# A conv feed-forward stage: one PSUM tile for each product accumulator, and casts, gelu and low parts issued at another distance from their users

## The chip, the cores and the metric

The kernel runs on one core of one Trainium2 chip. The metric is the time of one execution on the device in microseconds (us). Engines are named as in the profile: PE (TensorE, matmuls), PEld (its weight loads), DVE (VectorE), ACT (ScalarE), POOL (GpSimd; here it only issues transfers that add onto their target) and SP (SyncE, which issues plain transfers).

## The reference, cut to what matters

One layer of a diffusion backbone on 128 context tokens and 512 latent tokens, 640 in all, with a model width of 1024. Only the second half of the layer, the convolutional feed-forward, is touched:

```python
def _conv_ffn(h, w_up, w_dw, b_dw, w_down, latent):
    a, g = jnp.split(h @ w_up, 2, axis=-1)      # w_up (1024, 2 * 2816)
    ...                                         # conv: 3x3 depthwise on the latent grid, width 3 on the context
    conv = conv + b_dw
    return (jax.nn.gelu(conv) * g) @ w_down     # w_down (2816, 1024)

def _layer(x, cond, latent, s0_f, s0_b, alpha, p):
    ...                                         # token mixers, first norm, modulation: h2
    f = _conv_ffn(h2, p['w_up'], p['w_dw'], p['b_dw'], p['w_down'], latent)
    x = _layer_norm(alpha * x + g2 * f.astype(x.dtype), p['ln2_g'], p['ln2_b'])
```

## The kernel before

Activations lie with channels on partitions and the 640 tokens along the free axis. The 2816 channels are 22 tiles of 128, numbered j. For each j the stage needs an `a` and a `g` tile. Every operand of a product is kept as a rounded high part and a low part (what the rounding left), and a product is three matmuls (`mm3`, L277 to L279): high by high, high by low, low by high. The high part is a cast on ACT, the low part a subtraction on DVE (`low`, L195); `split` makes both, one right behind the other.

**Pairs.** Tiles 4 to 21 go through `up_pair`, which computes `a` and `g` of one j together with seven half-size products in place of eight (a Strassen-Winograd form on 512-row halves of the weights and 320-token halves of the activations). Each product is 12 matmuls of 128x320. Three accumulators take them: `xx` (products 1, 3, 5 and 7, all summed onto one another, with a copy to SBUF after each), `yy` (product 2) and `vv` (products 4 and 6). `xx` and `yy` are the two banks of one two-bank tile `pp`, `vv` is a one-bank tile. Between products the function issues the copies (ACT), the sums (DVE), a few operations of an older tile's convolution (`pump`) and one step of the weight preparation (`advance`).

**Weights.** A pair needs four quarters, named `a`, `c`, `r` and `t`, each split into a high tile `wh` and a low tile `wl`, with four buffers each. Pair j prepares the quarters of pair j + 1, one after the second, fourth, sixth and seventh product. The sums of weights that the seven products need are made by transfers: SP loads the raw tiles `ra` and `rb` of a pair (`load_pair`, called when `t` of the pair two before has been split) and a raw tile for `r`, and POOL issues transfers that add: two onto `rb`, then `ra[s] += rb[s]` when `a` has been split, from which `t` is cast. There are four such raw tiles (`sraw`), so two pairs' worth. A queue's transfers are issued in program order, and POOL's wait for the transfers before them where they read their result.

**Convolution.** `feed(j)` queues the operations of a tile's depthwise convolution: `begin` (an activation on ACT), ten taps on DVE, `close` (the gelu on ACT), then `gated` (a multiplication on DVE and a cast on ACT) and `rest` (the low part on DVE). `pump(n)` issues n of them. A pair issues 12, and a convolution has 12, so the queue keeps the length that it had.

**Down-projection.** After tiles 7, 9 and 14 a block (`down_part`) multiplies finished tiles by `w_down` and adds the result onto `x1d` in DRAM through POOL; it also prepares the next pair's quarters. Blocks for tiles 0 to 3, 4 to 7 and 8 to 13 stand between pairs; that for 14 to 21 comes last.

The order of instructions on all five engines is the order of the program text in this stage (a manual schedule), so where a line stands decides what it waits behind.

Of the kernel before, what the change touches and what calls it, by code (L numbers as in the profile page):

```python
# [18 lines left out]
P = 128  # L19
# [134 lines left out]
def layer_kernel(ctx, tc, wst, wada, par, cst, ftab, ttab, cond, x, state, sgub, wst_t, rows, bg, y, snew):  # L154
# [1386 lines left out]
    with tc.tile_pool(name="pu", bufs=1, reuse_waits="tile") as pu:  # L1541
        def onto(o, i):
            nc.gpsimd.dma_start(out=o, in_=i, accum_op=ALU.add)
# [34 lines left out]
        def next_pair():  # L1578
            if rest_pair:
                load_pair(rest_pair.pop(0))  # L1580

        def entry(key):
            kind, *a_ = key
            if kind == "a":
                ra, rb = pairs[a_[0]]
                got_w[key] = split(ra)
                onto(ra[:, s_], rb[:, s_])
            elif kind == "c":
                got_w[key] = split(pairs[a_[0]][1])
            elif kind == "t":  # L1590
                got_w[key] = split(pairs.pop(a_[0])[0][:, s_], 512)
                next_pair()
            else:
                w = got_w[key] = split(raws.pop(key))
                if kind == "d":
                    got_w[key] = halves(w)
                next_raw()

        def advance():
            if entries:  # L1600
                entry(entries.pop(0))
# [18 lines left out]
        def feed(j, at):  # L1620
# [23 lines left out]
            def close():  # L1644
                cv = hold["cv"]
                A.activation(cv, cv, AF.Gelu_apprx_tanh)  # L1646
                tail_q.extend([gated, rest])
                age[0] = 0

            def gated():  # L1650
# [15 lines left out]
        def pump(n):  # L1666
            while n and (taps_q or tail_q):
                if tail_q and (age[0] >= 2 or not taps_q):
                    tail_q.pop(0)()
                    age[0] = 0  # L1670
                else:
                    f = taps_q.pop(0)
                    f()
                    if f.__name__ in ("begin", "close"):
                        continue
                    age[0] += 1
                n -= 1

# [4 lines left out]
        def up_pair(j):  # L1683
            at = a, g = up_tiles(j)
            wa, wc, wr, wt = [(e, j) for e in "acrt"]
            pp = ppt("up")
            xx, yy, vv = pp[:, 0, 0:320], pp[:, 1, 0:320], p1t("up")[:, 0:320]

# [10 lines left out]
            V.tensor_tensor(a[:, near], a[:, near], yy, op=ALU.add)  # L1699
            pump(1)  # L1700
            product(xx, wc, 512, s2, 0)
            A.copy(g[:, near], xx)
# [3 lines left out]
            advance()  # L1706
            pump(1)
            product(xx, wr, 0, s3, 0)
            A.copy(g[:, far], xx)
# [5 lines left out]
            V.scalar_tensor_tensor(g[:, near], g[:, near], -1.0, vv, op0=ALU.mult, op1=ALU.subtract)  # L1715
            pump(1)
            product(xx, wt, 0, a22, 0)
            A.copy(a[:, far], xx)
            advance()
            pump(3)  # L1720
            feed(j, at)

        def up_one(j):
            at = up_tiles(j)
            for i in range(2):
                pp = ppt("up")
                for _ in proj_steps(pp, std[i], h2):
                    pass
                A.copy(tv(at[i]), pv(pp))
                pump(5)  # L1730
                advance()
            feed(j, at)

        def down_part(n):
# [5 lines left out]
            for nh in range(2):  # L1740
                for t in range(NT):
# [10 lines left out]
                    onto(x1d[t][:, c], ftmp)  # L1752
                    pump(rate)

        def contract(pr, ws, t, c0, cn, accum=None):
# [18 lines left out]
        with tc.manual_schedule(engines=MANUAL3 | {mybir.EngineType.Pool, mybir.EngineType.SP}):  # L1774
# [5 lines left out]
            advance()  # L1780
            advance()
            next_raw()
            for kind, n in jobs:
# [6 lines left out]
            while entries:  # L1790
                advance()
            for t in range(4):
                load_acc(t)
# [104 lines left out]
```

## Time and profile before

| | us |
|---|---|
| median of 3 runs (1368.27 to 1371.88) | 1370.25 |
| the profiled execution | 1375.1 |
| its span | 1373.3 |
| PE busy | 1225.7 |
| DVE busy | 892.0 |
| ACT busy | 512.6 |
| POOL busy | 91.9 |

The span is cut into 40 slices of 34.3 us on the page. The page's line of the granted clock gives, for each slice, the share of TensorE's full clock that it was allowed. The feed-forward's pairs run from 804 to 1304 us of the span.

### The profile page before, as it was taken

What the parts mean: (1) busy time and instruction counts of PE and PEld (TensorE: products, weight loads), DVE (VectorE), ACT (ScalarE), POOL (GpSimd) and SP (SyncE); (2) the same over time, 40 slices, a digit from 0 to 9 for tenths busy, and PEclk for the clock granted to TensorE, in tenths of its full rate; (3) what the DMA queues carried; (4) which work ended last, traced back from release to release, by engine and by line L of the source; (5) the groups of instructions that cost most, each with busy time, mean ns of one, the idle gap of its engine ahead of it and who ended that gap; (6) DMA issues with size and microseconds to landing.
All of it is one profiled execution on the core that took longest, in us unless ns stands there. A gap on an engine that the chain in (4) does not pass through costs nothing. (4 is left out here: it accounts for less than half of the span.)

```text
span 1373.3 us, 19086 instructions
## 1 busy us (share of the span) xinstructions
PE 1225.7 (89%) x7535; PEld 1151.2 (84%) x7535; DVE 892.0 (65%) x1656; ACT 512.6 (37%) x844; POOL 91.9 (7%) x111
## 2 busy tenths in 40 slices
PE   8999999999999999999999957888876897676897
PEld 7999999999999998999888856867776776675776
DVE  6697576486774858884678556675645553555586
ACT  5576363343433222322356333424233322333330
POOL 0000000000000000000000021021321022211000
PEclk9999999999999999999999968898986799676799
DMA  8412121121351525443432355575764347533242
GB/s 320 174 66 74 63 77 47 66 66 62 108 190 48 191 97 175 138 154 109 151 108 93 100 122 130 140 136 137 130 152 124 101 107 145 129 90 91 63 144 92
DMA packets 54970, 161.80 MB, mean 118 GB/s; under 512 B 6232, under 2 KB 8664, under 8 KB 54880
## 3 DMA queue, kind: packets, MB, share of 16 engines
q1 hardware_dynamic: 39472, 131.22, 28.0%
q0 software_dynamic: 15408, 29.37, 12.8%
q8 instruction: 59, 0.97, 0.3%
q14 instruction: 31, 0.25, 0.1%
HBM read 136.97 MB, written 14.16 MB: 110 GB/s over the span
## 5 line engine op out<-in xcount | busy, mean ns | idle before, releaser
L195 DVE TENSOR_TENSOR wl<-raw,wh 128x1024 fp32r<-128x1024 f32 x123 | 148.1, 1205 | 105.8 <-ACT wh L219 104.6
L277 PE MATMUL up<-go,wh 128*128 128x320 f32 (+2 forms) x384 | 138.4, 361 | 67.9 <-ACT fm L1695 60.3
L219 ACT CAST wh<-raw 128x1024 fp32r<-128x1024 f32 x119 | 122.8, 1034 | 198.3 <-PE gm L278 91.5
L277 PEld LDWEIGHTS up<-go,wh 128*128 128x128 f32 x384 | 87.2, 227 | 74.3 <-ACT fm L1695 65.1
L195 DVE TENSOR_TENSOR wl<-sraw,wh 128x1024 fp32r<-128x1024 f32 (+1 forms) x54 | 56.3, 1045 | 134.9 <-ACT wh L219 134.8
L278 PE MATMUL up<-go,wh 128*128 128x320 f32 (+2 forms) x384 | 134.3, 350 | 1.1 <-DVE go L195 1.1
L279 PE MATMUL up<-go,wl 128*128 128x320 f32 (+2 forms) x384 | 133.7, 348 | 0.5 <-DVE wl L195 0.5
L277 PE MATMUL up<-s,wh 128*128 128x320 f32 x216 | 79.9, 370 | 54.5 <-DVE fm L1699 54.5
L277 PE MATMUL gm<-h,wh 128*128 128x320 f32 x384 | 121.4, 316 | 0.0
L278 PE MATMUL gm<-h,wh 128*128 128x320 f32 x384 | 118.9, 310 | 0.0
L279 PE MATMUL gm<-h,wl 128*128 128x320 f32 x384 | 118.6, 309 | 0.0
L1641 DVE SCALAR_TENSOR_TENSOR cv<-fm,par,cv 128x441 f32<-128x441 f32 (+2 forms) x152 | 105.3, 692 | 2.3
L277 PEld LDWEIGHTS up<-s,wh 128*128 128x128 f32 x216 | 49.1, 227 | 60.8 <-DVE fm L1699 60.8
L421 DVE SCALAR_TENSOR_TENSOR adac<-rawa,csil,adac 128x512 f32<-128x512 f32 x120 | 84.8, 745 | 10.8 <-DMA rawa<-in_wada 8.8
L278 PEld LDWEIGHTS up<-go,wh 128*128 128x128 f32 x384 | 87.0, 227 | 2.4 <-DVE go L195 2.0
L279 PEld LDWEIGHTS up<-go,wl 128*128 128x128 f32 x384 | 86.0, 224 | 0.8 <-DVE wl L195 0.8
L219 ACT CAST wh<-sraw 128x1024 fp32r<-128x1024 f32 (+1 forms) x54 | 48.8, 905 | 82.6 <-DMA sraw<-sraw 30.9
L279 PE MATMUL up<-s,wl 128*128 128x320 f32 x216 | 77.1, 357 | 0.0
L278 PE MATMUL up<-s,wh 128*128 128x320 f32 x216 | 77.1, 357 | 0.0
L277 PE MATMUL dn<-wh,h 128*128 128x512 f32 (+1 forms) x188 | 72.6, 386 | 3.1 <-ACT h L1654 3.0
L279 PE MATMUL dn<-wh,h 128*128 128x512 f32 (+1 forms) x188 | 72.0, 385 | 1.9 <-DVE h L195 1.7
L277 PEld LDWEIGHTS gm<-h,wh 128*128 128x128 f32 x384 | 72.1, 188 | 1.7 <-issue 1.2
(454 smaller groups left out, 3283.6 us busy)
## 6 DMA issues: line engine op xcount, KB each, us to landing
raw<-in_wst SPq DMA_DIRECT2D x134, 512.0 KB, 3.6
sraw<-in_wst SPq DMA_DIRECT2D x36, 512.0 KB, 4.9
rawa<-in_wada SPq DMA_DIRECT2D x32, 512.0 KB, 3.5
sraw<-sraw POOLq DMA_DIRECT2D x36, 256.0 KB, 3.4
wa<-in_wada SPq DMA_DIRECT2D x16, 512.0 KB, 7.4
x1d<-ftmp POOLq DMA_DIRECT2D x30, 256.0 KB, 4.0
sraw<-in_wst POOLq DMA_DIRECT2D x18, 256.0 KB, 4.1
raw<-in_wst POOLq DMA_DIRECT2D x18, 256.0 KB, 4.4
```

The lines of the kernel that those rows point to most:

```text
L195: V.tensor_tensor(out, src, hi.bitcast(F32), op=ALU.subtract)
L219: A.copy(wh[:, 0:n], r)
L277: PE.matmul(out, lhsT=l[0], rhs=r[0], start=start, stop=False, skip_group_check=onto)
L278: PE.matmul(out, lhsT=l[0], rhs=r[1], start=False, stop=False, skip_group_check=onto)
L279: PE.matmul(out, lhsT=l[1], rhs=r[0], start=False, stop=stop, skip_group_check=onto)
L421: MAC.scalar_tensor_tensor(acc_[:, cd], r[:, i], s_, acc_[:, cd], op0=ALU.mult, op1=ALU.add)
L1641: V.scalar_tensor_tensor(cg[:, r0:r1, c0:c1], ag[:, r0 + r - 1:r1 + r - 1, c0 + c - 1:c1 + c - 1], tap(r, c), cg[:, r0:r1, c0:c1], op0=ALU ...
```

## The change

`up_pair` takes `xx` from a two-bank tile as before, but `yy` from a one-bank tile of its own, as `vv`. `split` is no longer used for the pairs' quarters: `cast` issues the cast on ACT at once and puts the low part, with the transfers that follow it, into a list; `settle` issues what is in the list. `settle` is called at the start of each `advance` and at fixed places of `up_pair`, ahead of the next product. The gelu becomes an operation of the tail queue (`curve`) that is issued when three operations have gone by since the last tap, or at once when there are no taps left; the distance of `gated` and `rest` stays two. `begin` of the next tile is issued one tap earlier where the next entry of the queue is the last.

```diff
--- before.py
+++ after.py
@@ -1579,24 +1579,40 @@
             if rest_pair:
                 load_pair(rest_pair.pop(0))
 
+        lows = []
+
+        def cast(r, n=1024):
+            wh = strm.tile([P, 1024], F32R, tag="wh", bufs=4, name=nm("wh"))
+            wl = strm.tile([P, 1024], F32R, tag="wl", bufs=4, name=nm("wl"))
+            A.copy(wh[:, 0:n], r)
+            return (wh, wl), lambda: low(wl[:, 0:n], r, wh[:, 0:n])
+
         def entry(key):
             kind, *a_ = key
             if kind == "a":
                 ra, rb = pairs[a_[0]]
-                got_w[key] = split(ra)
-                onto(ra[:, s_], rb[:, s_])
+                got_w[key], f = cast(ra)
+                after = lambda: onto(ra[:, s_], rb[:, s_])
             elif kind == "c":
-                got_w[key] = split(pairs[a_[0]][1])
+                got_w[key], f = cast(pairs[a_[0]][1])
+                after = lambda: None
             elif kind == "t":
-                got_w[key] = split(pairs.pop(a_[0])[0][:, s_], 512)
-                next_pair()
+                got_w[key], f = cast(pairs.pop(a_[0])[0][:, s_], 512)
+                after = next_pair
             else:
-                w = got_w[key] = split(raws.pop(key))
-                if kind == "d":
-                    got_w[key] = halves(w)
-                next_raw()
+                w, f = cast(raws.pop(key))
+                got_w[key] = halves(w) if kind == "d" else w
+                after = next_raw
+            lows.append((f, after))
+
+        def settle():
+            while lows:
+                f, after = lows.pop(0)
+                f()
+                after()
 
         def advance():
+            settle()
             if entries:
                 entry(entries.pop(0))
 
@@ -1642,10 +1658,11 @@
                                        tap(r, c), cg[:, r0:r1, c0:c1], op0=ALU.mult, op1=ALU.add)
 
             def close():
-                cv = hold["cv"]
-                A.activation(cv, cv, AF.Gelu_apprx_tanh)
-                tail_q.extend([gated, rest])
+                tail_q.extend([(curve, 3), (gated, 2), (rest, 2)])
                 age[0] = 0
+
+            def curve():
+                A.activation(hold["cv"], hold["cv"], AF.Gelu_apprx_tanh)
 
             def gated():
                 cv = hold["cv"]
@@ -1665,15 +1682,20 @@
 
         def pump(n):
             while n and (taps_q or tail_q):
-                if tail_q and (age[0] >= 2 or not taps_q):
-                    tail_q.pop(0)()
+                if tail_q and (age[0] >= tail_q[0][1] or not taps_q):
+                    f = tail_q.pop(0)[0]
+                    f()
                     age[0] = 0
+                    n -= f.__name__ != "curve"
+                    continue
                 else:
                     f = taps_q.pop(0)
                     f()
                     if f.__name__ in ("begin", "close"):
                         continue
                     age[0] += 1
+                    if len(taps_q) > 1 and taps_q[1].__name__ == "begin":
+                        taps_q.pop(1)()
                 n -= 1
 
         def up_tiles(j):
@@ -1683,8 +1705,8 @@
         def up_pair(j):
             at = a, g = up_tiles(j)
             wa, wc, wr, wt = [(e, j) for e in "acrt"]
-            pp = ppt("up")
-            xx, yy, vv = pp[:, 0, 0:320], pp[:, 1, 0:320], p1t("up")[:, 0:320]
+            xx = ppt("up")[:, 0, 0:320]
+            yy, vv = (p1t("up")[:, 0:320] for _ in range(2))
 
             def product(o, w, c0, acts, new):
                 w = got_w[w]
@@ -1698,6 +1720,7 @@
             advance()
             V.tensor_tensor(a[:, near], a[:, near], yy, op=ALU.add)
             pump(1)
+            settle()
             product(xx, wc, 512, s2, 0)
             A.copy(g[:, near], xx)
             pump(2)
@@ -1705,6 +1728,7 @@
             A.copy(a[:, far], vv)
             advance()
             pump(1)
+            settle()
             product(xx, wr, 0, s3, 0)
             A.copy(g[:, far], xx)
             pump(1)
@@ -1714,10 +1738,12 @@
             advance()
             V.scalar_tensor_tensor(g[:, near], g[:, near], -1.0, vv, op0=ALU.mult, op1=ALU.subtract)
             pump(1)
+            settle()
             product(xx, wt, 0, a22, 0)
             A.copy(a[:, far], xx)
             advance()
             pump(3)
+            settle()
             feed(j, at)
 
         def up_one(j):
@@ -1729,6 +1755,7 @@
                 A.copy(tv(at[i]), pv(pp))
                 pump(5)
                 advance()
+                settle()
             feed(j, at)
 
         def down_part(n):
@@ -1751,6 +1778,7 @@
                     V.scalar_tensor_tensor(ftmp, p1, 1.0 / ALPHA, g2[:, cd, c], op0=ALU.mult, op1=ALU.mult)
                     onto(x1d[t][:, c], ftmp)
                     pump(rate)
+                    settle()
 
         def contract(pr, ws, t, c0, cn, accum=None):
             cd = 0 if t == 0 else 1
@@ -1779,6 +1807,7 @@
                 feed(j, [landed.pop((j, i)) for i in range(2)])
             advance()
             advance()
+            settle()
             next_raw()
             for kind, n in jobs:
                 {"one": up_one, "pair": up_pair, "down": down_part}[kind](n)
@@ -1789,6 +1818,7 @@
                         low(lo, s1_[k], hi)
             while entries:
                 advance()
+            settle()
             for t in range(4):
                 load_acc(t)
             ln = [[mt()[:, 0:512] for _ in range(2)] for _ in range(2)]
```

Three places show how instructions move. In the names `up` is a product accumulator, `go` and `s` are activations, `wh` and `wl` the weights' parts, `cv` the convolution's tile, `fm` the `a` and `g` tiles, `raw` and `sraw` the weights' raw tiles, `ftmp` an evicted block of the down-projection; the number behind the name tells buffers apart.

PE, pair 20, at the end of its first and the start of its second product; before:

```order
L278 MATMUL up_11332<-go_7642,wh_11230 128x320
L279 MATMUL up_11332<-go_7641,wl_11231 128x320
L277 MATMUL up_11332<-go_7689,wh_11230 128x320
L278 MATMUL up_11332<-go_7690,wh_11230 128x320
L279 MATMUL up_11332<-go_7689,wl_11231 128x320
```

and now:

```order
L278 MATMUL up_11348<-go_7642,wh_11246 128x320
L279 MATMUL up_11348<-go_7641,wl_11247 128x320
L277 MATMUL up_11349<-go_7689,wh_11246 128x320
L278 MATMUL up_11349<-go_7690,wh_11246 128x320
L279 MATMUL up_11349<-go_7689,wl_11247 128x320
```

The order is the same; the second product writes a tile of its own.

DVE, the end of pair 19 and the start of pair 20, from the low part of `r` on (L195 with `raw`); before:

```order
L195 TENSOR_TENSOR wl_11299<-raw_11022,wh_11298 128x1024
L1715 SCALAR_TENSOR_TENSOR fm_11198<-fm_11198,up_11200 128x320
L1641 SCALAR_TENSOR_TENSOR cv_11214<-fm_11057,par,cv_11214 128x448
L195 TENSOR_TENSOR wl_11320<-sraw_11044,wh_11319 128x512
L1641 SCALAR_TENSOR_TENSOR cv_11214<-fm_11057,par,cv_11214 128x7x63
L1652 TENSOR_TENSOR cv_11214<-cv_11214,fm_11058 128x640
L195 TENSOR_TENSOR h_11327<-cv_11214,h_11326 128x640
L1633 SCALAR_TENSOR_TENSOR cv_11347<-fm_11197,par,cv_11347 128x127 x2
L195 TENSOR_TENSOR wl_11364<-sraw_11184,wh_11363 128x1024
L1699 TENSOR_TENSOR fm_11330<-fm_11330,up_11332 128x320
```

and now (the gate is L1669, the first taps L1649, the add of `yy` L1721):

```order
L195 TENSOR_TENSOR wl_11315<-raw_11038,wh_11314 128x1024
L1657 SCALAR_TENSOR_TENSOR cv_11230<-fm_11071,par,cv_11230 128x7x63
L1669 TENSOR_TENSOR cv_11230<-cv_11230,fm_11072 128x640
L195 TENSOR_TENSOR h_11342<-cv_11230,h_11341 128x640
L195 TENSOR_TENSOR wl_11336<-sraw_11065,wh_11335 128x512
L1649 SCALAR_TENSOR_TENSOR cv_11364<-fm_11212,par,cv_11364 128x127 x2
L1721 TENSOR_TENSOR fm_11346<-fm_11346,up_11349 128x320
L1657 SCALAR_TENSOR_TENSOR cv_11364<-fm_11212,par,cv_11364 128x7x63
L195 TENSOR_TENSOR wl_11381<-sraw_11206,wh_11380 128x1024
```

The low part of `t` (L195 with `sraw`, 128x512) stood ahead of the last tap, the gate and the low part of `h`, and stands behind them; the low part of the next `a` (the last `wl` row) stood ahead of the add of `yy` and stands behind it and a tap. ACT's order at this place is the same as before: copy of product 7, cast of `t`, gelu, cast of `h`, copy of the next product 1.

POOL, the end of the third down-projection block and the start of pair 15; before:

```order
L1543 DMA raw_10633<-in_wst 128x512
L1543 DMA sraw_10647<-in_wst 128x512
L1543 DMA sraw_10647<-sraw_10647 128x512
L1543 DMA x1d_7123<-ftmp_10652 128x512
L1543 DMA sraw_10226<-sraw_10227 128x512
```

and now:

```order
L1543 DMA raw_10650<-in_wst 128x512
L1543 DMA x1d_7123<-ftmp_10656 128x512
L1543 DMA sraw_10661<-in_wst 128x512
L1543 DMA sraw_10661<-sraw_10661 128x512
L1543 DMA sraw_10243<-sraw_10244 128x512
```

The block's last output accumulate (`x1d` from `ftmp`) stood between the two accumulates onto `rb` and `ra[s] += rb[s]`, and now stands ahead of all three.

## Rows read from the trace of the kernel before

**Rows 1.** The page's granted clock of TensorE, 40 slices, tenths.

```profile
PEclk9999999999999999999999968898986799676799
```

**Rows 2.** Waits of PE, 804 to 1306 us: waiter, releaser: total us, times, longest.

```profile
PE up L277 <- ACT fm L1695: 60.3, 18, 8.7
PE up L277 <- DVE fm L1699: 54.5, 18, 4.5
```

**Rows 3.** Windows between casts of t: length, busy time by engine, PEclk, DMA share, GB/s.

```profile
803.94:865.56 61.62, 46.60 (x244) 45.15 (x245) 36.19 (x56) 24.91 (x40) 9.60 (x11) 0.77 0.49 117
1010.37:1027.44 17.07, 13.43 (x79) 13.17 (x80) 9.58 (x14) 6.52 (x10) 3.53 (x4) 0.90 0.64 146
1168.71:1186.76 18.05, 14.53 (x76) 14.13 (x77) 9.13 (x14) 6.41 (x10) 3.10 (x4) 0.78 0.53 116
1027.44:1073.67 46.23, 32.90 (x167) 31.57 (x166) 25.28 (x39) 15.76 (x24) 6.11 (x7) 0.74 0.43 108
1186.76:1257.92 71.16, 51.18 (x254) 49.18 (x253) 38.58 (x58) 23.62 (x37) 10.49 (x12) 0.71 0.46 111
916.42:939.05 22.63, 16.97 (x84) 16.33 (x84) 15.49 (x23) 7.70 (x13) 4.36 (x5) 0.77 0.62 136
991.00:1010.37 19.37, 15.54 (x84) 14.88 (x84) 7.30 (x10) 5.68 (x10) 4.39 (x5) 0.82 0.75 166
1143.11:1168.71 25.60, 15.86 (x96) 15.07 (x94) 9.03 (x11) 5.80 (x10) 5.64 (x7) 0.89 0.68 151
865.56:885.73 20.17, 15.15 (x83) 14.61 (x82) 12.36 (x20) 7.54 (x13) 1.73 (x2) 0.83 0.54 154
939.05:957.34 18.29, 13.78 (x73) 13.51 (x74) 10.76 (x17) 7.28 (x11) 1.73 (x2) 0.81 0.58 168
1073.67:1097.17 23.50, 16.83 (x83) 16.16 (x82) 12.54 (x20) 7.56 (x13) 1.73 (x2) 0.71 0.45 133
1257.92:1303.79 45.87, 32.55 (x167) 31.21 (x166) 25.42 (x39) 15.44 (x25) 0.86 (x1) 0.74 0.17 52
```

**Rows 4.** Timeline, end of pair 18, ACT, DVE and PE: start, duration, line, idle before.

```profile
1234.12 0.62 ACT L219 CAST wh<-sraw 128x512 fp32r<-128x512 f32 x1
...
1236.92 0.74 ACT L1646 ACTIVATE cv<-cv 128x640 f32<-128x640 f32 x1 [2.18 <-DVE cv L1641]
...
1237.69 0.83 DVE L1652 TENSOR_TENSOR cv<-cv,fm 128x640 f32<-128x640 f32 x1 [0.80 <-ACT cv L1646]
...
1238.55 0.72 ACT L1654 CAST h<-cv 128x640 fp32r<-128x640 f32 x1 [0.89 <-DVE cv L1652]
...
1239.18 0.42 ACT L1695 COPY fm<-up 128x320 f32<-128x320 f32 x1
...
1239.31 0.83 DVE L195 TENSOR_TENSOR h<-cv,h 128x640 fp32r<-128x640 f32 x1 [0.79 <-ACT h L1654]
...
1239.65 0.64 PE L277 MATMUL up<-go,wh 128*128 128x320 f32 x1 [4.14 <-ACT fm L1695]
```

**Rows 5.** Windows: one product after a gap, and two products late in a pair.

```profile
1239.65:1243.15 3.50, 3.50 (x12) 3.17 (x12) 1.18 (x3) 0.93 (x2) 0.94 (x2) 0.50 0.73 178
1254.08:1257.60 3.52, 3.52 (x26) 3.52 (x25) 3.48 (x6) 1.48 (x2) 0.00 (x0) 1.00 0.00 0
```

**Rows 6.** Timeline, pairs 10 and 11, SP, POOL and ACT.

```profile
1011.74 0.33 SPq L1560 DMA_DIRECT2D sraw<-in_wst  x1
...
1017.54 0.87 POOL L1543 DMA_DIRECT2D sraw<-in_wst  x1 [3.55 <-DVE cv L1641]
1022.54 1.79 POOL L1543 DMA_DIRECT2D sraw<-sraw  x2 [4.13 <-DMA sraw<-in_wst]
...
1027.44 0.62 ACT L219 CAST wh<-sraw 128x512 fp32r<-128x512 f32 x1 [0.34 <-DMA sraw<-sraw]
```

**Rows 7.** Transfers, 804 to 1306 us: issues, KB each, median us to landing.

```profile
raw<-in_wst SPq DMA_DIRECT2D x34, 512.0 KB, 3.6
sraw<-sraw POOLq DMA_DIRECT2D x33, 256.0 KB, 3.4
```

## The prediction

> **What bounds the kernel now.** I read the slices of the page first [rows 1]: TensorE is granted its full clock for 23 of 40 slices and then, from about 790 us on, between 0.6 and 0.9 of it. That second part is the feed-forward stage, and there TensorE waits in every one of its 18 pair steps at the same two places [rows 2]: before the second product of a pair for ACT's copy at L1695 (60.3 us in all) and before the third product for DVE's add at L1699 (54.5 us). Both waits come from one tile: `xx` and `yy` lie in the two halves of `pp`, so a write to one half waits for a read of the other.
>
> I then cut the stage at the casts of the quarter `t`, the last of the four weight quarters that a pair prepares for the next (S(j) is the cast for pair j). These marks are used below because a loop runs from one to the next. [rows 3] gives the 18 steps: 389.6 us together, 21.6 us a pair. One product is 12 matmuls, 1.76 us at 2.4 GHz and 3.50 us at 1.2 GHz [rows 5], so seven full-speed products are 12.3 us, and 9.3 us a pair are waiting or slow clock. The row of the two products after 1254.08 has the clock at 1.00, the row right after a 4.14 us gap has 0.50.
>
> The late pairs show why the copy comes so late [rows 4]: ACT casts `t` at 1234.12, then the gelu waits for the last convolution tap on DVE, the gate on DVE waits for the gelu, the cast of `h` on ACT waits for the gate, and only then, at 1239.18, ACT gets to the copy. TensorE resumes at 1239.65.
>
> **The change, part by part.** *Tiles.* `yy` gets its own one-bank tile. Product 2 no longer waits for the copy, and product 3 no longer for the add; it still waits for the copy, since it accumulates onto `xx`, but product 2 now lies between. Work removed or added: none (the counts on TensorE, ACT, POOL and SP are unchanged, and DVE's seven extra listed rows are taps no longer listed together). The second one-bank tile per pair takes one of four rotating buffers; its former holders were evicted a pair or some blocks earlier, so I price it at nothing; if the cover failed, the price would be one wait for DVE, at most the 54.5 us / 18 = 3.0 us a pair of [rows 2].
>
> *Casts and low parts.* Each low part now stands a tap later on DVE, after the add instead of ahead of it. The four prepared quarters are used a whole pair later, so TensorE does not see it. It does matter for transfers: in the late pairs the order rows show `t`'s low part behind the gate and the low part of `h`. The load of the second raw tile `rb` of pair j+2 overwrites what this low part reads, so it starts later.
>
> *Gelu.* In the late pairs ACT's order at the pair's end is unchanged: the queue of taps is empty by then, so `curve` is issued at once, without its three operations of distance. The chain of [rows 4] stays, though it now delays product 3, not product 2.
>
> So something else has to bound a pair, and I see three candidates. TensorE: 12.3 us. DVE: 38.58 us busy in three pairs, 12.9 a pair [rows 3], plus the gaps that its own order keeps, 0.80 for the gelu and 0.79 for the cast of `h` [rows 4] and about 0.3 for the next opening activation: 14.8 us. And a loop through the transfers: the cast of `t` needs `ra[s] += rb[s]`; POOL issues that only after both accumulates onto the `rb` of the pair after; these need that `rb` loaded; the load needs the previous `t`'s low part. Where the kernel before runs into this loop it can be read off [rows 6]: cast 1010.37, load of `rb` issued 1011.74, first accumulate 1017.54, second 1022.54, the third behind it at 1022.54 + 0.90, and the next cast starts on its landing at 1027.44. That is 17.07 us: 1.37 + 5.80 + 5.00 + 0.90 + 4.00. The other late steps, 22.5 to 23.9 us, hide it.
>
> With the new order of DVE, the first term grows. From the cast of `t`: 0.65 to the gelu, 0.77 to the gate (1236.92 to 1237.69), 0.86 to the cast of `h`, 0.76 to its low part, 0.75 until `t`'s low part starts and 0.68 that it takes: 4.5 us. The second term shrinks, because the loads ahead of `rb` are done by then: a load by itself lands after 3.6 us (median of the 512 KB raw loads, [rows 7]). Sum 4.5 + 3.65 + 5.00 + 0.90 + 4.00 = 18.05 us. With the load still at 5.80 it is 20.2; with the last landing at its median of 3.4 [rows 7] it is 17.4. I take 18.05, as the load then is nearest to one by itself. TensorE fits in: product 3 starts about 4.2 us after the cast, and products 3 to 7 take 3.50 + 2.9 + 3 x 1.76 = 11.7 us if the gap slows the first two, together 15.9.
>
> By the Trainium skill (DMA: Bandwidth & Descriptors, section on the anatomy of one DMA) a transfer costs about 2.0 us plus its bytes at 436 GB/s: 3.2 us for 512 KB and 2.6 us for 256 KB. By that estimate the loop would be 4.5 + 3.2 + 2.6 + 0.9 + 2.6 = 13.8 us and would bind nothing, which is the first rival below; the rows have 4.0 and 5.0 us for these 256 KB accumulates, and the measurement decides.
>
> The steps of [rows 3], before and after:
> - Five steps in which the loop and the late chain act together (1027.44 to 1073.67 and 1186.76 to 1257.92): 117.4 us, then 5 x 18.05 = 90.3. Gain 27.1.
> - Five steps with no gelu between cast and low part (three in 803.94 to 865.56, 1010.37 to 1027.44, 1168.71 to 1186.76): 96.7 us, then the loop as it was, 5 x 17.0. Gain 11.7.
> - Three steps from a down-projection block: 67.6 us. The last output accumulate now stands ahead of the weights' accumulates on POOL, not between them (order rows), which takes one transfer out of the loop; but `t`'s low part stands behind that block's eviction and, at pairs 8 and 10, two taps. Bounds: nothing, and 3 x 18 = 54, a gain of 13.6. I take 3, near the low end, because the two shifts oppose each other.
> - Five steps outside the loop, since no `t` behind them waits for a pair's load (865.56 to 885.73, 939.05 to 957.34, 1073.67 to 1097.17, and two in 1257.92 to 1303.79): 107.8 us. The first two keep no gelu in front of the copy: cast 0.62, opening activation 0.92, copy 0.42, 0.5 to restart, then five products, 8.8 us fast and 12.3 with two of them slow: 11.3 to 14.8, taken as 13 each. The other three take DVE's 14.8. Sum 70.4, gain 37.4.
>
> Total gain 79.2 us. The profiled execution took 1375.1 us for a span of 1373.3, 4.85 above the runs' median of 1370.25; the same distance below 1375.1 - 79.2 = 1295.9 gives **1291 us**. Down-projection blocks, the part before 804 us and the tail are taken as unchanged, since none of the two waits lies there and no product is added or moved.
>
> **The rivals.** *The transfers are quicker and the loop binds nothing.* Then DVE's 14.8 us bounds the first kind too (74 us), about 14 the second (70), the third gains its 13.6: 43.4 + 26.7 + 13.6 + 37.4 = 121.1, time 1249. For it: the loop's figures come from a stretch with DMA busy at 0.64, the late pairs have 0.43 to 0.46 [rows 3]. Against it: quicker pairs raise that share.
>
> *The loop gets longer*, because loads and accumulates crowd together: 20.2 us in the first kind, nothing gained in the second and third: 16.4 + 37.4 = 53.8, time 1317. For it: the 5.80 us in [rows 6].
>
> *TensorE stays at 1.2 GHz.* The only long gap per pair would now lie before product 3; if the clock fell there and did not come back within the pair, seven products would take 24.5 us and a pair some 25.5: 18 x 25.5 - 389.6 = 69 us slower, about 1440. It decides from 21.6 us a pair on. Against it: before the change two gaps a pair still leave 0.71 to 0.74 in these steps [rows 3], and the clock is back at 1.00 by the sixth product [rows 5].
>
> *The change does nothing*: product 3 waits for the same copy and takes over the whole wait. For it: the chain of [rows 4] is not shortened. Against it: product 2 now runs inside that wait, and the add's wait has no successor.
>
> **How the numbers follow.** My forecast 0.55 (1275 to 1308 for itself), quick transfers 0.25, long loop 0.13, no effect 0.03, slow clock 0.04. The range of 1250 to 1318 reaches to the first rival's time and to the long loop's; what it leaves out is half of the quick case and the last two. A measurement of this kernel tells about 0.3% from no change: faster 0.93, same 0.03, slower 0.04.
>
> **What would show it.** Right: no TensorE wait between a pair's first and second product; one wait per pair, before the third, for ACT's copy, of 2 to 3 us in the late pairs; ACT's cast of `t` waiting for `ra[s] += rb[s]` in most steps; casts of `t` 17 to 19 us apart; the load of `rb` issued some 4.5 us after the cast. Wrong: casts of `t` that wait for TensorE or DVE alone (the loop does not bind), steps of 20 us or more, a granted clock below 0.7 in the late steps, or down-projection blocks that change by more than 2 us.

## The result and the profile after

The changed kernel takes 1299.35 us (median of 4 runs, 1294.89 to 1306.42) against 1371.07 us for the kernel before (4 runs): a ratio of 0.948, 95% interval 0.9424 to 0.9536. Five more runs in another session gave 1306.41 us and 0.9502 (0.948 to 0.9524). The forecast was 1291 us with a range of 1250 to 1318. The profiled execution of the changed kernel took 1306.42 us (span 1304.6), 68.7 less than that of before; all sums below are made against this one.

The page's granted clock, and the waits of PE and ACT (waiter, line, releaser: total us, times, longest us), which answer to [rows 1, 2]:

```profile
PEclk9999999999999999999999997799898889888989
```

```profile
PE up L277 <- ACT fm L1717: 88.8, 17, 10.8
...
ACT wh L1587 <- DMA sraw<-sraw: 101.5, 15, 12.8
```

Two kinds of wait of 18 each have become one: nothing waits between a pair's first and second product, nothing waits for the add, and the third product waits for the copy of the first (L1717). That wait is longer than either was. The row of ACT says why: ACT's casts wait 101.5 us for landings of `sraw<-sraw`, and the copy stands on ACT behind the cast of `t`.

The twelve windows of [rows 3], between the same casts, in the same order:

```profile
799.80:856.47 56.67, 43.04 (x252) 42.38 (x252) 39.78 (x61) 23.32 (x39) 9.57 (x11) 0.83 0.56 132
994.37:1014.41 20.04, 14.62 (x84) 14.36 (x84) 11.12 (x17) 6.40 (x11) 3.52 (x4) 0.84 0.56 129
1130.10:1147.28 17.18, 14.98 (x84) 14.72 (x84) 11.12 (x17) 6.41 (x10) 2.63 (x3) 0.82 0.63 148
1014.41:1052.28 37.87, 27.93 (x168) 27.40 (x168) 25.09 (x38) 15.52 (x25) 5.23 (x6) 0.86 0.54 130
1147.28:1206.68 59.40, 42.27 (x249) 41.74 (x250) 37.78 (x57) 23.30 (x36) 10.46 (x12) 0.83 0.56 127
903.23:924.24 21.01, 14.12 (x84) 13.86 (x84) 15.45 (x23) 7.05 (x13) 3.48 (x4) 0.85 0.64 155
971.06:994.37 23.31, 12.74 (x86) 12.32 (x84) 7.30 (x9) 5.58 (x10) 5.39 (x7) 0.90 0.75 163
1109.57:1130.10 20.53, 15.80 (x108) 15.53 (x106) 7.28 (x9) 5.79 (x9) 5.24 (x6) 0.99 0.82 183
856.47:867.38 10.91, 9.23 (x62) 9.10 (x62) 9.40 (x15) 7.14 (x11) 0.87 (x1) 1.00 0.75 216
924.24:937.55 13.31, 11.70 (x61) 11.69 (x62) 9.33 (x16) 7.24 (x11) 1.73 (x2) 0.72 0.62 170
1052.28:1067.24 14.96, 11.71 (x61) 11.71 (x62) 10.88 (x18) 7.33 (x11) 1.73 (x2) 0.70 0.53 157
1206.68:1233.24 26.56, 22.34 (x150) 21.80 (x149) 22.66 (x36) 15.12 (x23) 0.85 (x1) 1.00 0.26 75
...
sum 321.75, PE 240.48 PEld 236.61 DVE 207.20 ACT 130.22 POOL 50.68; mean PE 20.04 PEld 19.72 DVE 17.27 ACT 10.85 POOL 4.22
```

The 18 steps take 321.75 us, 67.8 less than before, and that is nearly all of the 68.7. The remaining 0.9 is a balance: up to the first cast 4.1 less, the three down-projection blocks between pairs 1.4 more (111.69 against 110.29; the first grew by 5.2, the third shrank by 3.6), the tail 1.9 more.

Two turns of the loop on ACT, SP, POOL, DVE and PE, which answer to [rows 4, 6]: from the cast of `t` for pair 5 to that for pair 6, and from that for pair 17 to that for pair 18 and the third product behind it:

```profile
819.26 0.62 ACT L1587 CAST wh<-sraw 128x512 fp32r<-128x512 f32 x1 [6.10 <-DMA sraw<-sraw]
...
820.63 0.33 SPq L1560 DMA_DIRECT2D sraw<-in_wst  x1
...
828.91 0.87 POOL L1543 DMA_DIRECT2D sraw<-in_wst  x1 [8.07 <-DMA sraw<-in_wst]
833.33 1.75 POOL L1543 DMA_DIRECT2D sraw<-sraw  x2 [3.54 <-DMA sraw<-in_wst]
...
840.35 0.62 ACT L1587 CAST wh<-sraw 128x512 fp32r<-128x512 f32 x1 [7.61 <-DMA sraw<-sraw]
...
1147.28 0.62 ACT L1587 CAST wh<-sraw 128x512 fp32r<-128x512 f32 x1 [4.26 <-DMA sraw<-sraw]
...
1151.69 0.33 SPq L1560 DMA_DIRECT2D sraw<-in_wst  x1
1162.12 0.33 SPq L1569 DMA_DIRECT2D raw<-in_wst  x1
...
1156.78 0.87 POOL L1543 DMA_DIRECT2D sraw<-in_wst  x1 [6.79 <-DVE cv L1657]
1161.11 1.76 POOL L1543 DMA_DIRECT2D sraw<-sraw  x2 [3.46 <-DMA sraw<-in_wst]
1167.17 0.86 POOL L1543 DMA_DIRECT2D raw<-in_wst  x1 [4.30 <-DMA raw<-in_wst]
...
1167.88 0.62 ACT L1587 CAST wh<-sraw 128x512 fp32r<-128x512 f32 x1 [6.48 <-DMA sraw<-sraw]
...
1169.17 0.82 DVE L1669 TENSOR_TENSOR cv<-cv,fm 128x640 f32<-128x640 f32 x1 [6.48 <-ACT cv L1665]
...
1170.66 0.42 ACT L1717 COPY fm<-up 128x320 f32<-128x320 f32 x1
...
1171.13 0.63 PE L277 MATMUL up<-s,wh 128*128 128x320 f32 x1 [6.68 <-ACT fm L1717]
```

The second turn, read as the prediction read it: 4.41 from the cast to the load of `rb`, 5.09 to the first accumulate, 4.33 to the second, 0.88 to the third (the second of the `x2` row, taken at half of it), and 5.89 until the cast starts on its landing: 20.60 us. The row of the first accumulate names DVE as its releaser; by the trace the load of `rb` lands at 1156.20, which is when POOL's wait ends, and the row starts 0.58 us later. The load of `r` (L1569) is issued 0.13 us after the third accumulate and moves beside it. ACT, DVE and PE all stand still until the landing. The first turn, with the low part of `t` early, has 1.37, 8.28, 4.42, 0.88 and 6.14 us, together 21.09. Transfers from 800 to 1236 us (issues, KB each, median us to landing) against the second of [rows 7]; the accumulates have gone from 3.4 to 4.4:

```profile
sraw<-sraw POOLq DMA_DIRECT2D x33, 256.0 KB, 4.4
```

### The profile page after: what moved, and what is told of

It reads as the page before. It is cut to its first block, busy times and chain, and to the rows that moved or that the text cites. A ratio compares the mean times of both kernels' runs of the same rounds, so it can differ in the third digit from the quotient of the medians.

```text
span 1304.6 us, 19072 instructions
## 1 busy us (share of the span) xinstructions
PE 1184.2 (91%) x7535; PEld 1116.2 (86%) x7535; DVE 887.8 (68%) x1656; ACT 509.9 (39%) x844; POOL 91.7 (7%) x111
## 5 line engine op out<-in xcount | busy, mean ns | idle before, releaser
L195 DVE TENSOR_TENSOR wl<-raw,wh 128x1024 fp32r<-128x1024 f32 x123 | 148.0, 1204 | 84.9 <-ACT wh L219 75.9
L277 PE MATMUL up<-s,wh 128*128 128x320 f32 x216 | 76.8, 356 | 88.8 <-ACT fm L1717 88.8
L219 ACT CAST wh<-raw 128x1024 fp32r<-128x1024 f32 x83 | 85.0, 1027 | 168.3 <-PE gm L278 91.6
L277 PE MATMUL up<-go,wh 128*128 128x320 f32 (+2 forms) x384 | 124.2, 323 | 7.3 <-ACT fm L1755 6.3
L278 PE MATMUL up<-go,wh 128*128 128x320 f32 (+2 forms) x384 | 123.1, 321 | 1.0 <-DVE go L195 1.0
L279 PE MATMUL up<-go,wl 128*128 128x320 f32 (+2 forms) x384 | 122.3, 318 | 0.4 <-DVE s11hv L307 0.4
L195 DVE TENSOR_TENSOR wl<-sraw,wh 128x1024 fp32r<-128x1024 f32 (+1 forms) x54 | 56.3, 1043 | 73.5 <-ACT wh L1587 73.1
L1587 ACT CAST wh<-sraw 128x1024 fp32r<-128x1024 f32 (+1 forms) x54 | 48.7, 903 | 127.4 <-DMA sraw<-sraw 101.5
L277 PEld LDWEIGHTS up<-go,wh 128*128 128x128 f32 x384 | 76.8, 200 | 8.8 <-ACT fm L1755 6.6
L278 PEld LDWEIGHTS up<-go,wh 128*128 128x128 f32 x384 | 76.2, 199 | 2.4 <-DVE go L195 2.0
L279 PEld LDWEIGHTS up<-go,wl 128*128 128x128 f32 x384 | 75.8, 197 | 0.8 <-DVE s11hv L307 0.8
L278 PE MATMUL up<-s,wh 128*128 128x320 f32 x216 | 74.2, 343 | 0.0
L279 PE MATMUL up<-s,wl 128*128 128x320 f32 x216 | 73.9, 342 | 0.0
L277 PEld LDWEIGHTS gm<-h,wh 128*128 128x128 f32 x384 | 72.1, 188 | 1.7 <-issue 1.2
```

The costliest lines, as they stand in the source:

```text
L195: V.tensor_tensor(out, src, hi.bitcast(F32), op=ALU.subtract)
L219: A.copy(wh[:, 0:n], r)
L277: PE.matmul(out, lhsT=l[0], rhs=r[0], start=start, stop=False, skip_group_check=onto)
L278: PE.matmul(out, lhsT=l[0], rhs=r[1], start=False, stop=False, skip_group_check=onto)
L279: PE.matmul(out, lhsT=l[1], rhs=r[0], start=False, stop=stop, skip_group_check=onto)
L1587: A.copy(wh[:, 0:n], r)
```

## The experiments

My theory: the changed kernel's steps are set by the transfer loop, and TensorE's remaining wait is only where this shows. Rivals: the tiles or the order alone set what is gained, or the landings are slow wherever they stand. Ratios are to the kernel before in the same session.

**The two halves of the change, each alone.** The edit of the first run, in the kernel before:

```diff
-            pp = ppt("up")
-            xx, yy, vv = pp[:, 0, 0:320], pp[:, 1, 0:320], p1t("up")[:, 0:320]
+            xx = ppt("up")[:, 0, 0:320]
+            yy, vv = (p1t("up")[:, 0:320] for _ in range(2))
```

> The kernel before with only the three product accumulators of a pair in tiles of their own; casts, gelu and low parts stay in the old order. Theory: the late steps of the changed kernel are set by the transfer loop (cast of t, low part of t, load of the right half, three accumulating transfers, landing), and in the old order the low part of t stands right behind its cast, 0.6 + 0.7 us instead of 4.4 us, so a late step is 20.8 - 3.1 = 17.7 us unless the old order's waits between ScalarE and VectorE hold it: 1265 to 1290 us, below the changed kernel. Rival, the order carries part of the gain: without it the waits of VectorE for casts and gelu keep the add and the evictions late, and the steps stay over 19 us in every pair: 1305 to 1340 us.

Measured: 1310.54 us, ratio 0.9566 (0.9542 to 0.9591).

The second run takes the same lines back out of the changed kernel.

> The changed kernel with the first two products of a pair back in the two halves of one tile; the new order of casts, gelu and low parts stays. Theory: the second and the third product wait again for the copy and the add, TensorE keeps falling to half clock, and the gain is lost: 1345 to 1375 us. Rival, the order by itself brings the copy and the add so much earlier that the shared tile costs little: 1300 to 1330 us.

Measured: 1312.28 us, ratio 0.9582 (0.9552 to 0.9612). Both times lie in the rivals' ranges: each half alone gives some 60 us, and both together, by the ratios, only 0.6 to 1.0% more. The first rival's mechanism did not show: with the tiles alone the steps do not stay over 19 us everywhere. Three late ones, from the cast for pair 17 to that for pair 20, take 51.01 us, where the changed kernel has 59.40 in the windows above:

```profile
1157.69:1208.70 51.01, 40.65 (x236) 40.12 (x237) 37.73 (x56) 23.60 (x36) 10.49 (x12) 0.83 0.63 145
```

Waits in the tiles-only kernel and then in the order-only kernel:

```profile
ACT wh L219 <- DMA sraw<-sraw: 72.1, 12, 12.7
...
PE up L277 <- ACT fm L1695: 67.9, 14, 10.6
```

```profile
ACT wh L1587 <- DMA sraw<-sraw: 45.2, 12, 12.0
...
PE up L277 <- DVE fm L1721: 11.7, 18, 1.2
```

In both, ACT's casts wait for landings (45.2 and 72.1 us; before it was 30.9). In the second the tile is still shared, yet the wait for the add has fallen from the 54.5 of [rows 2] to 11.7.

**Which part of the order.** In the order-only kernel, gelu and opening activation go back to their old places; only the low parts stay later:

```diff
-                tail_q.extend([(curve, 3), (gated, 2), (rest, 2)])
+                cv = hold["cv"]
+                A.activation(cv, cv, AF.Gelu_apprx_tanh)
+                tail_q.extend([gated, rest])
...
-                    if len(taps_q) > 1 and taps_q[1].__name__ == "begin":
-                        taps_q.pop(1)()
```

> Of the new order only the low parts behind the cast by a few operations; the gelu and the opening activation stand as in the kernel before, and the first two products share a tile. Theory: what the order by itself gained (1312 us in place of 1370) came from the low part of a, which stood on VectorE ahead of the add that frees the tile for the third product and waited for its cast; with it behind the add the wait for the add falls from 3.0 to below 1 us a pair and the time is that of the whole order: 1306 to 1320 us. Rival, the gelu's and the opening activation's new places carry it: 1340 to 1372 us.

Measured: 1312.46 us, ratio 0.9587 (0.9543 to 0.963), the theory. DVE in a pair of the kernel before, and PE behind it:

```profile
1244.07 1.23 DVE L195 TENSOR_TENSOR wl<-sraw,wh 128x1024 fp32r<-128x1024 f32 x1 [2.88 <-ACT wh L219]
1245.21 0.48 DVE L1699 TENSOR_TENSOR fm<-fm,up 128x320 f32<-128x320 f32 x1
...
1245.75 0.64 PE L277 MATMUL up<-s,wh 128*128 128x320 f32 x1 [2.53 <-DVE fm L1699]
```

And in this run:

```profile
1170.98 0.49 DVE L1715 TENSOR_TENSOR fm<-fm,up 128x320 f32<-128x320 f32 x1 [1.88 <-PE up L279]
...
1171.97 1.22 DVE L195 TENSOR_TENSOR wl<-sraw,wh 128x1024 fp32r<-128x1024 f32 x1
...
1171.52 0.64 PE L277 MATMUL up<-s,wh 128*128 128x320 f32 x1 [0.58 <-DVE fm L1715]
```

Before, the low part of `a` stood ahead of the add and waited 2.88 us for its cast; now the add starts on the product that it reads, and PE's wait is 0.58 instead of 2.53.

**The loop opened.** In the changed kernel the two accumulates into `rb` are kept back and issued on POOL behind the next `ra[s] += rb[s]`:

```diff
-            onto(rb[:, f_], wst[ia][:, f_])
-            onto(rb[:, s_], rb[:, f_])
+            late.append((j, lambda: [onto(rb[:, f_], wst[ia][:, f_]), onto(rb[:, s_], rb[:, f_])]))
+
+        def catch_up(j):
+            while late and late[0][0] <= j:
+                late.pop(0)[1]()
...
-                after = lambda: onto(ra[:, s_], rb[:, s_])
+                catch_up(a_[0])
+                after = lambda: [onto(ra[:, s_], rb[:, s_]), catch_up(NF)]
```

> The changed kernel with the two accumulates into the right half of pair j+2 issued on POOL behind the third accumulate of pair j+1 instead of ahead of it; nothing else moves. Theory (the loop sets the late steps because the third accumulate is queued behind transfers of a pair later): the third accumulate no longer hangs on the loads that the cast of t releases, no cast of t waits for a landing, and a step falls to what VectorE has to do in a pair, some 14 us, or to a little more, 15 to 17 us: 1215 to 1260 us. Rival, the landings themselves are the limit (bandwidth shared by seven transfers a pair), wherever they stand in the queue: steps over 19 us, 1280 to 1300 us.

Measured: 1248.33 us, ratio 0.9111 (0.9078 to 0.9143), the theory, but for three casts of `t` that still wait for a landing (0.5, 2.0 and 7.2 us), all within two steps behind a down-projection block. Two steps between casts of `t`, and PE's wait for the copy:

```profile
1117.58:1132.19 14.61, 12.58 (x86) 12.32 (x85) 12.91 (x21) 7.78 (x13) 3.45 (x4) 1.00 0.80 184
1132.19:1146.40 14.21, 12.59 (x86) 12.32 (x85) 12.51 (x20) 7.77 (x14) 3.46 (x4) 1.00 0.82 189
```

```profile
PE up L277 <- ACT fm L1721: 27.1, 11, 5.9
```

A step is down to 14.2 to 14.6 us at a clock of 1.00, with DVE busy for 12.5 to 12.9 of it. DMA is busier (0.80 to 0.82 against 0.56 in the three late steps from 1147.28 us), so the bandwidth of the DMA engines was not what held the late steps.

**The halves with the loop open.** The same edit in the kernel before, then in it with the tiles alone, and in the changed kernel with the shared tile.

> The kernel before, old tiles and old order, with the accumulates into the right half of pair j+2 issued on POOL behind the third accumulate of pair j+1. Theory: in the kernel before the shared tile sets the steps (some 21.6 us a step with TensorE at half clock), and the transfer loop is hidden behind it, so freeing it gives little: 1345 to 1370 us. Rival, the loop held the kernel before as well, and the tile only shared the blame: 1290 to 1330 us.

Measured: 1373.56 us, ratio 1.001 (0.9995 to 1.0025): nothing.

> Tiles of their own and the later accumulates, old order of casts, gelu and low parts. Theory: with the loop gone, what the order is worth can be seen: in the old order VectorE waits in each pair for the casts and the gelu right ahead of it (some 1 us for each of four, beside 12.4 us of its own work), a step of 16 to 17 us instead of 14.2: 1270 to 1300 us against 1248 with both parts. Rival, the order is worth nothing once tiles and accumulates are mended: 1244 to 1255 us.

Measured: 1287.51 us, ratio 0.9389 (0.9357 to 0.9421).

> The new order and the later accumulates, with the first two products in the two halves of one tile. Theory: the waits for the copy and the add come back, steps of 17 to 19.5 us with TensorE partly at half clock: 1285 to 1312 us. Rival, with the new order the copy and the add come early enough that the shared tile is free by the time TensorE asks for it: 1244 to 1260 us.

Measured: 1292.74 us, ratio 0.9433 (0.9398 to 0.9468). In the last two the theory; in the first its mechanism, with the time 3.6 us over its range. PE's waits in the first of them are those of [rows 2] again, though ACT waits for one landing only:

```profile
ACT wh L219 <- DMA sraw<-sraw: 13.7, 1, 13.7
...
PE up L277 <- DVE fm L1704: 62.5, 18, 7.3
PE up L277 <- ACT fm L1700: 55.1, 18, 10.3
```

As ratios to the kernel before, and so free of the session:

| | transfers as before | accumulates later |
|---|---|---|
| neither half | 1 | 1.001 |
| tiles alone | 0.9566 | 0.9389 |
| order alone | 0.9582 | 0.9433 |
| both | 0.948, 0.9502 | 0.9111 |

On the right the tiles bring 3.2% on top of the order (0.9433 to 0.9111) and the order 2.8% on top of the tiles. On the left each brings about 1% or less on top of the other.

**The last landing.** In the changed kernel, r of pairs 16 to 21 is neither loaded nor summed:

```diff
+                if a_[0] > 15:
+                    raws[key] = one[0]
+                    return
                 r = raws[key] = strm.tile([P, 1024], F32, tag="raw", name=nm("raw"))
+                one[:] = [r]
```

> The changed kernel without the load and the accumulate of r for pairs 16 to 21 (they all use the r of pair 15, so their results differ); the four steps from the cast of t of pair 16 to that of pair 20 then have no raw transfer beside the third accumulate. Theory: the third accumulate took 5.9 to 6.7 us instead of 4.0 because the load of r, 512 KB, moved at the same time: it falls back to about 4 us and these steps to 18.0 to 19.0 us each. Rival 1: the second accumulate, issued 0.9 us ahead on the same queue, is what it shares with: the landing stays at 5.9 to 6.7 us and the steps at 20 to 21 us.

Measured: 1298.82 us, ratio 0.9467 (0.9423 to 0.9512). POOL and ACT, the second and third accumulate and the cast:

```profile
1156.91 1.75 POOL L1543 DMA_DIRECT2D sraw<-sraw  x2 [3.49 <-DMA sraw<-in_wst]
...
1161.76 0.62 ACT L1591 CAST wh<-sraw 128x512 fp32r<-128x512 f32 x1 [3.07 <-DMA sraw<-sraw]
...
1175.20 1.74 POOL L1543 DMA_DIRECT2D sraw<-sraw  x2 [3.78 <-DMA sraw<-in_wst]
...
1180.06 0.62 ACT L1591 CAST wh<-sraw 128x512 fp32r<-128x512 f32 x1 [3.98 <-DMA sraw<-sraw]
```

Taken at half of each `x2` row, 0.87 us in, the third accumulate is followed by the cast after 3.98 and 3.99 us; the steps behind the four unloaded quarters are 16.98, 17.82, 18.30 and 18.62 us, where the changed kernel has 17.18, 20.60, 21.07 and 17.73. The landing is settled for the theory. The run takes the accumulate of `r` away with the load; in the turn shown above that one was issued at 1167.17, 0.71 us ahead of the cast, so it is the load that moved beside the landing nearly throughout. The four steps save 4.9 us in the profiles; the times do not tell that from nothing.

**The changed kernel again**, for a second profile:

> The changed kernel once more, unaltered, for a second profile and more times. Theory (the transfer loop sets the steps, and its landings differ from run to run): the late steps whose third accumulate shares with a load are again 20 us or more, and the sum of the casts' steps again accounts for the time: 1294 to 1306 us. Rival, the profiled run was an exception: no late step over 19 us.

Measured: 1306.41 us, 1303.0 to 1307.85. The theory, with the median 0.4 us over its range and one of the late steps just under 20: from pair 17 to 20 they are 21.03, 20.85 and 19.76 us, the first of them:

```profile
1145.05:1166.08 21.03, 14.13 (x84) 13.87 (x84) 12.60 (x19) 7.78 (x13) 4.20 (x5) 0.92 0.57 128
```

**The low part of t earlier**, `settle()` ahead of the pair's last `pump(3)`:

```diff
             advance()
-            pump(3)
             settle()
+            pump(3)
```

> The changed kernel with the low part of t issued right behind its cast, ahead of the last three operations of the convolution queue of a pair. Theory (the loop sets the late steps): from the cast of t to the end of its low part 1.3 us instead of 4.4, so each of some 13 steps that end on a landing gets up to 3 us shorter: 1265 to 1285 us. Rival, the load then only stands longer behind other work (the queue of POOL, landings that share bandwidth) and the landing of the third accumulate stays where it was: 1294 to 1304 us.

Measured: 1295.1 us, ratio 0.9462 (0.9417 to 0.9508), within the rival's range; against the changed kernel it can't be told from no change. The loop from pair 16 to 17, ACT, SP, POOL and ACT:

```profile
1128.45 0.62 ACT L1587 CAST wh<-sraw 128x512 fp32r<-128x512 f32 x1 [7.69 <-DMA sraw<-sraw]
...
1128.44 0.33 SPq L1559 DMA_DIRECT2D sraw<-in_wst  x1
1129.82 0.33 SPq L1560 DMA_DIRECT2D sraw<-in_wst  x1
...
1134.91 0.87 POOL L1543 DMA_DIRECT2D sraw<-in_wst  x1 [8.26 <-DVE cv L1657]
1139.29 1.76 POOL L1543 DMA_DIRECT2D sraw<-sraw  x2 [3.51 <-DMA sraw<-in_wst]
...
1145.11 0.62 ACT L1587 CAST wh<-sraw 128x512 fp32r<-128x512 f32 x1 [3.96 <-DMA sraw<-sraw]
```

The first term is 1.37 us, but the load of `rb` is now issued 1.38 us behind that of `ra` and takes 5.09 to its accumulate; 16.66 in all. The late steps did fall, to between 16.4 and 17.3 us, but steps of 20 to 21 us elsewhere stayed, and the whole gained no more than the runs' scatter.

**Beyond the change.** Two kernels with the loop open. In the first, the low part of `t` as in the run above:

> Both parts of the change, the later accumulates, and the low part of t right behind its cast. Theory: with the loop gone VectorE's own order sets a step: 12.4 us of work and two waits of 0.8 us, for the gelu and for the cast of h; the low part of t, 0.7 us, now fills one of them: 13.5 us a step instead of 14.2, 1232 to 1244 us. Rival, the cast of t with its low part then delays the gelu by as much as it fills: 1245 to 1251 us.

Measured: 1258.07 us, ratio 0.916 (0.9133 to 0.9186): neither; its good steps take 14.2 us as without it, and others 16 to 17 at a clock of 0.9. Why these came back was not followed. In the second, the convolution is queued ahead of the last `pump(3)` as well, by moving `feed(j, at)` up:

> As the run before, and a pair's convolution is queued ahead of the last three operations of the pair, so that the gelu, the gate and the low part of the tile before always have taps of the next tile between them. Theory: VectorE's two waits of 0.8 us a pair go, a step falls to 12.5 to 13 us, near TensorE's own 12.3: 1218 to 1235 us. Rival, the opening activation and the first taps now wait for the last product of the pair, and VectorE loses there what it wins: 1236 to 1260 us.

Measured: 1246.41 us, ratio 0.907 (0.9047 to 0.9094), the rival's range: steps of 13.9 us, not told apart from the 0.9111 of the open loop alone. This kernel and the one with the loop open and nothing else moved are the fastest here.

## Why the prediction was right, and where not

**The bound.** The forecast rested on the loop replacing TensorE's two waits, and that is shown: opening the loop takes the changed kernel from ratios of 0.948 and 0.9502 to 0.9111, some 51 to 54 us, and nothing off the kernel before. The first rival (transfers quick enough to hide, 1249 us) is what the opened loop makes, at 1248.33; in the changed kernel they did not hide. That the two times agree so closely is luck: in that run the 18 steps take some 254 us where the rival had 268.5, and the three down-projection blocks some 13 us more than in the kernel before. The Trainium skill's fit (DMA: Bandwidth & Descriptors, anatomy of one DMA), by which a turn would take an estimated 13.8 us, does not agree: 5.09 us were measured where it has 3.2 for the load, and 4.33 and 5.89 where it has 2.6 for an accumulate (3.98 with no load beside it), and the choice of the rows over the page held. The Trainium skill gives that fit for transfers that GpSimd issues, and SP issues the load of `rb`, so the 3.2 us stretch it.

**The sum**, by its own four kinds of step:

| steps | before | predicted | measured |
|---|---|---|---|
| five, loop and late chain | 117.4 | 90.3 | 97.3 |
| five, no gelu between cast and low part | 96.7 | 85.0 | 93.9 |
| three from a down-projection block | 67.6 | 64.6 | 64.9 |
| five outside the loop | 107.8 | 70.4 | 65.7 |
| all | 389.6 | 310.4 | 321.75 |

The miss of 11.4 us is made of +7.0, +8.9, +0.3 and -4.7. With the 0.9 gained elsewhere the profiled time is 10.5 over the 1295.9 that the prediction worked out for it; this run lay 7.1 above its median instead of the 4.9 assumed, and so 1299.35 stands against 1291.

**First kind: the last landing was mis-sized.** Of 4.5 + 3.65 + 5.00 + 0.90 + 4.00 the measured turn has 4.41, 5.09, 4.33, 0.88 and 5.89. The first and fourth term were right, the second and third are off by +1.4 and -0.7, and the last by +1.9 us. The run without the load of `r` brings it back to 3.98 and the three steps of this kind to 17.8 to 18.6, about the predicted 18.05. The 4.00 of [rows 6] was carried over without asking what would move beside that landing once the steps are shorter.

**Second kind: the same landing.** The prediction kept 17.0 us a step from one turn. Steps of this kind now range from 16.12 to 21.09 us. Read as in the turn above, the terms add up over the five steps of each kind to (us):

| term | first kind, predicted | first kind, measured | second kind, as in [rows 6] | second kind, measured |
|---|---|---|---|---|
| cast to load of `rb` | 22.5 | 22.0 | 6.9 | 6.9 |
| load to first accumulate | 18.3 | 21.0 | 29.0 | 30.5 |
| first to second | 25.0 | 22.5 | 25.0 | 23.8 |
| second to third | 4.5 | 4.4 | 4.5 | 4.4 |
| third to the next cast | 20.0 | 27.4 | 20.0 | 28.4 |

So the last landing makes up nearly all of what both kinds are over; the other terms nearly cancel. It goes with the moment at which the next raw tile is loaded: over these ten turns and the same ten of the second profile, the last term is 5.37 to 6.72 us in the thirteen where such a load is issued less than 2 us behind the third accumulate or just ahead of it, and 4.13 to 5.59 in the seven where it comes later. In the longest step the load term, 5.80 in [rows 6], is 8.28 as well: the load of `rb` leaves right behind that of `ra`. In the run with the low part of `t` earlier, the load term grows by 9.2 us over the five steps of the first kind and so eats most of the 13.4 us that their first term saves.

**Fourth kind.** 65.7 instead of 70.4: the steps after which no loop follows came to 10.9 to 15.0 us, the last two together 26.6, at a clock of 1.00.

**Tiles against order.** The prediction gave the tiles all of the gain and the order only a price, the longer first term; of the low parts it says that TensorE does not see them. This step failed. The low parts leaving the add's way are alone worth 59 us with the shared tile, and the order is worth 2.8% with the loop open; the gelu's and the opening activation's places are worth nothing that can be measured with the shared tile (1312.46 against 1312.28). The price is there too: with the tiles alone the five steps of the first kind take 85.3 us, with both parts 97.3 (99.0 in the second profile). Against it, the three stretches that hold a down-projection block (856.47 to 924.24, 924.24 to 994.37 and 1052.28 to 1130.10) take 215.7 us with both parts (215.0) and 229.9 with the tiles alone; why was not followed. With the transfers as before, the order's gain and its price thus nearly cancel. That the forecast survived the failed step is luck: either half is enough to run into the loop, for before, steps of 21.6 us hid a loop of 17.07 [rows 6] to about 21 us.

**The signs.** No wait between the first and second product, one before the third, the load of `rb` 4.4 us after the cast, and casts that wait for `ra[s] += rb[s]`: all there. That third product's wait of 2 to 3 us was wrong (6.68 here, 88.8 / 17 = 5.2 on average), because the copy that it waits for stands on ACT behind the cast, and so waits for the landing too; late steps went to 21 us, a sign set down for "wrong", and two down-projection blocks moved by more than 2 us, in opposite directions. TensorE's clock stayed at 0.70 or more in every window above, so the slow-clock rival had nothing.

## What to carry to other kernels

Before crediting a gain to an edit, look for the next limit behind the one that it removes: here two edits above one floor each seem to bring nearly everything, and only opening the floor showed that both count. A loop through transfers is read off the trace term by term, and each term needs a look at what else moves in that stretch. Where a queue is in order, issue what the nearest user waits for ahead of work for a pair later, even if that work is ready to be queued first; this pays only once the queue is what binds, as the same edit in the kernel before brought nothing.

## What was not expected of the hardware

One 256 KB accumulate within on-chip memory, issued 0.9 us behind another, landed after 3.98 us with no load beside it and after 5.89 us with a 512 KB load issued 0.13 us later, while the DMA engines were busy for only 0.56 of these steps.
